# Retention matmuls in three rounded passes, a group norm split over three engines, and a merge projection that opens with a pair

## The chip, the cores and the metric

One core of a Trainium2 chip runs the whole layer. TensorE (PE) multiplies, VectorE (DVE) and ScalarE (ACT) do elementwise work, GpSimd (POOL) a little of it, and SyncE (SP) issues most of the DMAs. The metric is device time in microseconds (us) of one execution, lower is better. Three runs of the kernel before gave 1579.16, 1580.39 and 1580.98 us.

## The reference, cut to what matters

The layer works on 1024 positions of width 1024, in float32:

```python
h = rms_norm(x); proj = h @ w_in          # q, k, v, gates, two LRU branches, two merge gates
# branch A: retention, 4 heads, dk 128, dv 256; per chunk:
scores = (q_i @ k_i.T) * intra_decay
out    = scores @ v_i + (q_i * q_decay) @ state
state  = state * chunk_decay + (k_i * k_decay).T @ v_i
# per head: group norm over the 256 values of a position, times silu(gate), then @ w_ret_o
y = (o - mean(o)) * rsqrt(var(o) + GN_EPS)
# branch B: causal conv, RG-LRU (gates, scan), times gelu, then @ w_lru_o
mix = sigmoid(gA) * y_a + sigmoid(gB) * y_b
x = x + mix @ w_out                       # the merge projection
# gated MLP: h2 @ w_up (1024 x 6144), causal conv of width 3, gelu * val, @ w_down (3072 x 1024)
return rms_norm(x + ...)
```

The kernel handles two chunks of 64 positions as one block of 128, with a mask that holds the decays.

## The kernel before, in words

**Products.** The large products run with operands split by `split` (lines 465 to 471) into a rounded part and the rest, both of type float32r (written fp32r): ACT casts (L469), DVE subtracts (L470). A product of two split operands takes three passes, `PASSES = ((0, 0), (0, 1), (1, 0))`: high times high, high times low, low times high. A pass is one PE instruction, 128x512 in most places. On top of that the 2x2 blocks of a projection are multiplied by a Strassen-Winograd scheme: seven block products (`A11, S1, S2, A12, S3, A22, S4` against `B11, T1, T2, B21, T3, T4, B22`) instead of eight, at the price of sums of blocks on DVE. `mm_fast` does the seven (L718), `mm_by` does the plain eight (L680). A block product is 4 column groups of 3 passes, 12 instructions. A job with `mate` runs as a pair: each block of the right side is used by two jobs in turn.

**Stages.** First come the values of the retention heads (`values`, L1454), then the other input projections in the order of the string `SEQ`. The work on their results is written as generators (`back`, `builders`) that are advanced between block products: `rotary_head`, `retention_head` and `ret_out` for the heads, `lru_block` for branch B. Then follow the two output projections, the merge projection (`wjobs`, four jobs of 256 rows, `t` from 0 to 3), the up projection (`ups`) with its conv, and the down projection (`djobs`), whose last job ends in `final_half`.

**Retention.** Per head there are eight blocks. Each block makes three products in plain float32: scores transposed (L1233, 128x128), scores times values (L1239, 128x256) with the state's share added in the same bank (L1241), and, but for the last block, the state's update (L1250, 128x256). Between them DVE applies the mask (L1236) and the state's decay (L1254), ACT copies the result out (L1246). In the trace every float32 product stands as two PE instructions. After four blocks the group norm follows: DVE statistics (L1258, L1259), `rstd_of` (ACT square root L826, then a reciprocal and four small DVE operations with one Newton step), and one DVE operation per block that applies it (L1265).

**Merge projection.** Job `t=0` is plain (eight block products, by `mm_by` with the inner half as the outermost loop); the jobs 1 to 3 are fast. The right side is read in eight sets: the four blocks of `w_out` and the four sums, which an earlier stage left in DRAM as `tw_d`.

**Start and end.** The first eight columns of the parameters come by a DMA of POOL's queue (L1478), one tile of the input by ACT's queue, all else by SP's. Twelve matmuls on a zeroed tile `heat` run ahead (L1484). At the end the last quarter of the output is done in two halves of 256 columns by `final_half` (L1886 to L1906): a sum of squares (L1892), its addition (L1893), a multiplication by the norm's weights (L1894), then a power on POOL (L1897) and two scalings.

**What sets the order.** The program is built twice. The first build gives a list of instructions and their dependencies; the class `Plan` works out due times backward (`latest`), then picks instructions forward engine by engine (`forward`) with its own costs, and the second build is chained to that order. In `forward`, DVE and ACT may be left idle for an instruction that is soon ready (constants `NEAR`, `APART`).

Of the kernel before, what the change touches and what calls it, by code (L numbers as in the profile page):

```python
# [18 lines left out]
P = 128  # L19
# [180 lines left out]
class Plan:  # L200
# [8 lines left out]
    NEAR, APART = 500.0, 10000.0  # L209
# [97 lines left out]
    def forward(self, rank):  # L307
# [17 lines left out]
        while left:  # L325
# [100 lines left out]
def tile_trunk_layer(ctx, tc, x, xt, positions, params, consts, normf, w_in, w_v, w_ro, w_lo,  # L426
# [11 lines left out]
    sm = Units(pool, "sm", 4, [P, P], now)  # L438
# [386 lines left out]
    def rstd_of(dst, var, tmp):  # L825
        S.activation(tmp, var, AF.Sqrt)  # L826
        V.reciprocal(dst, tmp)
        V.tensor_mul(tmp, dst, dst)
        V.tensor_mul(tmp, tmp, var)
        V.tensor_scalar(tmp, tmp, -0.5, 1.5, ALU.mult, ALU.add)  # L830
        V.tensor_mul(dst, dst, tmp)

# [352 lines left out]
    def rotary_head(hd, qk):  # L1185
# [12 lines left out]
        for h in range(2):  # L1198
            ps = psa.get()
            for b in range(4):  # L1200
                bs = slice(128 * b, 128 * b + 128)
                PE.transpose(ps[:, bs], qk[1, h][:, bs], ident)
            t = get()
            for b in range(4):
                bs = slice(128 * b, 128 * b + 128)
                n = 4 * h + b
                S.activation(t[:, bs], ps[:, bs], AF.Copy, scale=kdr[:, hd, n:n + 1])
            psa.put(ps)
            kd[h] = t
            yield 0.5  # L1210
# [6 lines left out]
    def retention_head(hd, qk):  # L1217
        cur = 0
        tick = now[0]
        for g in range(2):  # L1220
            vt[0, g] = v_tile(hd, 0, g)
        yield from landed(tick)
        mask = cst[:, C_MASK + 128 * hd:C_MASK + 128 * hd + 128]
        for h in range(2):
            for b in range(4):
                if h == 0 and b % 2 == 0:
                    vt[1, b // 2] = v_tile(hd, 1, b // 2)
# [3 lines left out]
                v = vt[h, b // 2][:, 256 * (b % 2):256 * (b % 2) + 256]  # L1231
# [5 lines left out]
                psa.put(p1)  # L1237
                p2 = psa.get()
                PE.matmul(p2[:, 0:256], s, v, start=True, stop=first)  # L1239
                if not first:  # L1240
                    PE.matmul(p2[:, 0:256], qk[0, h][:, bs], rst[cur], start=False, stop=True)  # L1241
                sm.put(s)
# [168 lines left out]
    def values():  # L1411
# [74 lines left out]
        for j in (1, 2, 3):  # L1486
            wload("A11", j)
            xload("B11", j)
# [397 lines left out]
    def final_half(u, s):  # L1886
# [8 lines left out]
        if s.start == 0:  # L1895
            return
# [114 lines left out]
```

## Time and profile before

| | |
|---|---|
| runs | 1579.16, 1580.39, 1580.98 us (median 1580.39) |
| profiled execution | 1579.13 us, its span 1577.3 us |
| PE busy | 1566.6 us, 99% of the span, 7013 matmuls |
| DVE busy | 1373.0 us, 87% |
| ACT busy | 933.9 us, 59% |
| POOL busy | 52.6 us, 3% |
| granted clock of PE | 0.999 |

The profile is one execution. Its parts that are used below: the busy times by engine; groups of instructions by line and shape (count, busy time together, mean ns of one, and the idle time of the engine before them); the list of waits; the chain of work that ended last; the timeline; and busy times by stretch of the span. A matmul's shown duration is longer than its turn on PE, since matmuls overlap; its turn is read from the distance between starts, or from the busy time of a run of them.

### The profile page before, as it was taken

The numbers are of one execution on the slowest core, as the hardware profiler recorded it, in microseconds if no ns is written. First come the engines' busy times: TensorE is split into PE (matmuls) and PEld (weight loads), VectorE is DVE, ScalarE is ACT, GpSimd is POOL, SyncE is SP. The second block draws the span as 40 slices with busy tenths as digits, with TensorE's granted clock in tenths as the row PEclk, the third lists the DMA queues.
The fourth block names the chain that finished last, engine by engine and source line by source line (L and its number), as shares of the span: only waits on it lengthen the run. The fifth ranks groups of instructions, "written<-read, shape, count | busy, mean of one in ns | idle before, by whom it ended". The sixth has DMA issues, their size and how long they took to land.

```text
span 1577.3 us, 21478 instructions
## 1 busy us (share of the span) xinstructions
PE 1566.6 (99%) x7013; PEld 1294.2 (82%) x7013; DVE 1373.0 (87%) x2470; ACT 933.9 (59%) x1586; POOL 52.6 (3%) x74
## 2 busy tenths in 40 slices
PE   9999999999999999999999999999999999999998
PEld 7888888888888888888888888888888888888887
DVE  8999988898899888999997899777777778987885
ACT  7547964655567696955365764444444446563653
POOL 0001000000000000000000001000000000000000
PEclk9999999999999999999999999999999999999999
DMA  9344334444454245684996246444444456787752
GB/s 324 114 127 140 127 127 152 136 154 168 124 178 153 75 146 180 225 276 162 306 376 233 92 123 218 134 143 140 138 138 138 139 190 218 256 284 269 262 181 87
DMA packets 159328, 282.11 MB, mean 179 GB/s; under 512 B 17256, under 2 KB 29680, under 8 KB 159216
## 3 DMA queue, kind: packets, MB, share of 16 engines
q1 hardware_dynamic: 153664, 264.74, 51.1%
q0 software_dynamic: 4256, 13.64, 2.9%
q10 hardware_dynamic: 1296, 2.36, 0.4%
q8 instruction: 55, 0.90, 0.2%
q14 instruction: 57, 0.47, 0.1%
HBM read 195.73 MB, written 83.89 MB: 177 GB/s over the span
## 4 chain that ended last, share of the span: by engine, by line
PE 90%; DVE 4%; ACT 3%; DMA 1%; issue 1%; POOLq 0%; ACTq 0%; DVEq 0%; SPq 0%
PE g L718 78%; PE g L1454 5%; PE a L1130 2%; PE g L680 1%; DVE w L470 1%; PE a L1239 1%; PE a L1241 1%; PE a L1250 1%; PE a L1233 0%; PE a L1300 0%; DMA u<-td_d 0%; PE a L1720 0%; ACT u L469 0%; DMA u<-w_dn 0%; DMA w<-mix_d 0%
## 5 line engine op out<-in xcount | busy, mean ns | idle before, releaser
L718 PE MATMUL g<-u,w 128*128 128x512 f32 x5976 | 1390.1, 391 | 1.6 <-ACT u L767 1.5
L718 PEld LDWEIGHTS g<-u,w 128*128 128x128 f32 x5976 | 1115.2, 188 | 231.9 <-ACT u L767 3.5
L469 ACT CAST w<-w 128x512 fp32r<-128x512 f32 x516 | 316.6, 621 | 355.3 <-PE g L718 254.8
L470 DVE TENSOR_TENSOR w<-w,w 128x512 fp32r<-128x512 f32 x516 | 349.1, 682 | 63.3 <-ACT w L469 57.7
L747 DVE TENSOR_TENSOR u<-g,u 128x512 f32<-128x512 f32 x213 | 145.4, 684 | 52.9 <-PE g L718 43.7
L469 ACT CAST u<-u 128x512 fp32r<-128x512 f32 x233 | 138.4, 620 | 56.9 <-PE g L718 5.4
L767 ACT COPY u<-g 128x512 f32<-128x512 f32 x215 | 124.9, 582 | 61.6 <-PE g L718 59.4
L470 DVE TENSOR_TENSOR u<-u,u 128x512 fp32r<-128x512 f32 x233 | 152.8, 681 | 3.3 <-ACT u L469 2.8
L1769 DVE SCALAR_TENSOR_TENSOR u<-u,par,u 128x511 f32<-128x511 f32 x96 | 71.2, 743 | 2.9 <-ACT u L1766 2.6
L1454 PE MATMUL g<-w,u 128*128 128x512 f32 x264 | 61.9, 390 | 1.2 <-DVE u L1439 1.0
L1454 PEld LDWEIGHTS g<-w,u 128*128 128x128 f32 x264 | 49.3, 188 | 12.3 <-issue 1.5
L1774 POOL DMA_DIRECT2D ff_d<-u x48 | 36.1, 752 | 451.5 <-DVE u L1773 451.5
L1130 PE MATMUL a<-u,u 128*128 128x512 f32 x192 | 50.7, 393 | 0.3 <-ACT u L469 0.2
L555 DVE TENSOR_TENSOR w<-w,w 128x512 f32<-128x512 f32 x71 | 48.4, 682 | 1.4 <-DMA w<-w_lo 0.7
L558 DVE TENSOR_TENSOR w<-w,w 128x512 f32<-128x512 f32 x71 | 48.5, 684 | 0.9
L561 DVE TENSOR_TENSOR w<-w,w 128x512 f32<-128x512 f32 x71 | 48.4, 682 | 0.3
L564 DVE TENSOR_TENSOR w<-w,w 128x512 f32<-128x512 f32 x71 | 48.4, 682 | 0.3
L1766 ACT ACTIVATE u<-u,par 128x512 f32<-128x512 f32 x48 | 39.2, 816 | 16.0 <-DVE u L747 15.9
L741 DVE TENSOR_TENSOR u<-u,u 128x512 f32<-128x512 f32 x45 | 30.9, 686 | 16.9 <-ACT u L767 16.6
L1130 PEld LDWEIGHTS a<-u,u 128*128 128x128 f32 x192 | 35.5, 188 | 9.3 <-ACT u L469 1.3
L1773 DVE TENSOR_TENSOR u<-u,u 128x512 f32<-128x512 f32 x48 | 32.8, 686 | 6.1 <-ACT u L1772 6.1
L1112 DVE SCALAR_TENSOR_TENSOR u<-u,par,u 128x511 f32<-128x511 f32 (+2 forms) x48 | 35.7, 743 | 2.4 <-ACT u L1108 2.2
(211 smaller groups left out, 1130.4 us busy)
## 6 DMA issues: line engine op xcount, KB each, us to landing
w<-w_in SPq DMA_DIRECT2D x96, 256.0 KB, 2.7
w<-w_up SPq DMA_DIRECT2D x96, 256.0 KB, 2.7
u<-w_dn SPq DMA_DIRECT2D x84, 256.0 KB, 3.8
u<-x_d SPq DMA_DIRECT2D x60, 256.0 KB, 4.3
x_d<-u SPq DMA_DIRECT2D x48, 256.0 KB, 3.6
ff_d<-u POOLq DMA_DIRECT2D x48, 256.0 KB, 2.7
td_d<-u SPq DMA_DIRECT2D x48, 256.0 KB, 3.0
u<-td_d SPq DMA_DIRECT2D x48, 256.0 KB, 4.8
```

The costliest lines, as they stand in the source:

```text
L469: S.copy(hi, src)
L470: V.tensor_sub(lo, src, hi.bitcast(F32))
L555: V.tensor_add(s, r["A21"], r["A22"])
L558: V.tensor_sub(s, s, r["A11"])
L561: V.tensor_sub(s, r["A12"], s)
L564: V.tensor_sub(src, r["A21"], r["A11"])
L718: PE.matmul(bank[:, s], w[a][:, c], need(op, (SETS[nm], j))[b][:, s], start=first and n == 0, stop=n == 11, skip_group_check=True)
L747: V.tensor_add(u, bank, u)
L767: S.copy(u, bank)
L1130: PE.matmul(ps, wg[g][a][:, cs], xs[k][b], start=q == 0, stop=q == 5)
L1454: PE.matmul(bank, o[p][:, c], w[q], start=first and j == n == 0, stop=j == 3 and n == 2, skip_group_check=True)
L1769: V.scalar_tensor_tensor(c[:, s:], src[:, :TH - s], w, c[:, s:], ALU.mult, ALU.add)
```

## The change

1. In the retention, scores times values and the state's update take three rounded passes instead of one float32 product. For that the masked scores are split (128x128, per block), the values (four tiles per head) and the scaled keys (two tiles per head; the second half is made later, by the new `keys`). The scores themselves and the state's share stay in float32.
2. The group norm: `rstd_of` goes. POOL raises the variance to the power -0.5, DVE makes minus the mean times that, and ACT applies both as scale and bias.
3. The merge projection's first two jobs run as a fast pair in the order `FIRST`, and the right side is read in seven sets.
4. The first parameters and a second input tile go by ACT's queue; the zeroed tile is a unit of the common pool, given back after use.
5. In `final_half` the addition of the sum of squares is chained ahead of the multiplication by the weights.
6. The plan's rule for leaving DVE or ACT idle is another: an instruction is put off when a more urgent one gets ready before it would end.

```diff
@@ Plan.forward
-    NEAR, APART = 500.0, 10000.0
+    MARGIN, EXTRA = 600.0, 2000.0
             if e in ("DVE", "Activation"):
-                soon = min(((rank[n], at) for at, n in wait[e] if at < t + self.steps[item[1]].hold + self.NEAR),
-                           default=None)
-                if soon and soon[0] < min(t, item[0] - self.APART):
+                cost = self.steps[item[1]].hold
+                if e == "Activation" and switch(item[1]):
+                    cost += self.SWITCH
+                soon = min(((rank[n], at, self.steps[n].hold) for at, n in wait[e] if at < t + cost), default=None)
+                if soon and soon[0] < t + cost + self.MARGIN and item[0] > soon[1] + soon[2] + self.EXTRA:
                     free[e] = soon[1]
                     continue
@@ retention_head
+        def v_split(h, g):
+            t = raw.pop((h, g))
+            vt[h, g] = split(t)
+            put(t, late=SOONER)
...
+                s = s, *split(s, sm.get)
                 p2 = psa.get()
-                PE.matmul(p2[:, 0:256], s, v, start=True, stop=first)
+                for n, (i, j) in enumerate(PASSES):
+                    PE.matmul(p2[:, 0:256], s[1 + i], v[j][:, vs], start=n == 0, stop=first and n == 2)
...
-                    PE.matmul(p3[:, 0:256], kd[h][:, bs], v, start=True, stop=True)
+                    for n, (i, j) in enumerate(PASSES):
+                        PE.matmul(p3[:, 0:256], kd[h][i][:, bs], v[j][:, vs], start=n == 0, stop=n == 2)
...
-            rstd_of(rs[:, 1, :], rs[:, 0, :], rs[:, 2, :])
+            G.tensor_tensor(rs[:, 1, :], rs[:, 0, :], half[:, 0:4], ALU.pow)
+            V.scalar_tensor_tensor(rs[:, 2, :], mv[:, :, 0], -1.0, rs[:, 1, :], ALU.mult, ALU.mult)
             for b in range(4):
                 o = ob[h, b // 2][:, 256 * (b % 2):256 * (b % 2) + 256]
-                V.tensor_scalar(o, o, mv[:, b, 0:1], rs[:, 1, b:b + 1], ALU.subtract, ALU.mult)
+                S.activation(o, o, AF.Identity, bias=rs[:, 2, b:b + 1], scale=rs[:, 1, b:b + 1])
@@ keys (new; the loop over both halves stood in rotary_head)
+    def keys(hd, qk, h):
...
+        kd[h] = split(t)
+        put(t, late=SOONER)
@@ values
-        G.dma_start(par[:, 0:8], params[:, 0:8])
+        nc.scalar.dma_start(par[:, 0:8], params[:, 0:8])
         xload("B11", 0, nc.scalar)
+        xload("B11", 1, nc.scalar)
@@ merge projection
-        builders.append(operand(wop, w_out_set, False))
-        builders.append(kept_sums(wop, tw_d))
+        builders.append(operand(wop, kept_or(w_out_set, tw_d), False, ("B11", "T3", "B21", "T1", "T2", "T4", "B22")))
...
-                 emit_out(t, t > 0), out_post(t), fast=t > 0, last=t == 3, drop12=t == 0,
-                 pre=((0, 0), (0, 1), (1, 1)), fetch=from_x(t), by=None if t else "k",
-                 order=None if t else ("A11", "A21", "A12", "A22"),
+                 emit_out(t, True), out_post(t), fast=True, last=t == 3,
+                 pre=((0, 0), (0, 1), (1, 1)), fetch=from_x(t), mate=t == 0, prods=FIRST if t < 2 else PRODS,
@@ final_half
-        V.tensor_add(one, one, two)
-        V.tensor_mul(o[:, s], u[:, s], nf[1][:, s])
+        a = V.tensor_add(one, one, two)
+        b = V.tensor_mul(o[:, s], u[:, s], nf[1][:, s])
         if s.start == 0:
             return
+        tc.add_manual_dep(b.ins, a.ins.name, mybir.DependencyInfo(mybir.DependencyClass.NoSync,
+                          mybir.DependencyReason.DATA), reason="the sum first")
```

What the plan makes of it is shown at two places. PE in the first head, before: `a` are the two PSUM banks of the small products, `g` those of the projections, `sm` the masked scores.

```order
L1233 MATMUL a_89_2649<-u_417_2234,u_418_2271 128x128
L718 MATMUL g_79_2274<-u_268_860,w_427_2290 128x512
L718 MATMUL g_82_2337<-u_205_605,w_432_2310 128x512
L718 MATMUL g_82_2337<-u_206_606,w_432_2310 128x512
L718 MATMUL g_82_2337<-u_205_605,w_433_2311 128x512
L718 MATMUL g_82_2337<-u_209_614,w_432_2310 128x512
L1239 MATMUL a_91_2653<-u_437_2550,sm_15_2651 128x256
L1241 MATMUL a_91_2653<-state_87,u_417_2234 128x256
L1250 MATMUL a_93_2657<-u_437_2550,u_433_2498 128x256
```

The same block with the change (L1239 is now the scores, L1247 their product with the values, L1249 the state's share, L1259 the state's update, L720 the projections):

```order
L1239 MATMUL a_95_2749<-u_419_2234,u_420_2271 128x128
L720 MATMUL g_85_2441<-u_183_495,w_449_2375 128x512
L720 MATMUL g_85_2441<-u_182_494,w_450_2376 128x512
L720 MATMUL g_85_2441<-u_184_504,w_449_2375 128x512
L720 MATMUL g_85_2441<-u_185_505,w_449_2375 128x512
L720 MATMUL g_85_2441<-u_184_504,w_450_2376 128x512
L1259 MATMUL a_99_2764<-u_467_2705,u_461_2655 128x256
L1259 MATMUL a_99_2764<-u_468_2706,u_461_2655 128x256
L1259 MATMUL a_99_2764<-u_467_2705,u_462_2656 128x256
L1247 MATMUL a_97_2757<-u_467_2705,sm_44_2753 128x256
L1247 MATMUL a_97_2757<-u_468_2706,sm_44_2753 128x256
L720 MATMUL g_85_2441<-u_186_514,w_449_2375 128x512
```

The state's update moved ahead of the product that waits for the scores, and that product's third pass, which needs the low part of the scores (`sm_45`), stands one projection matmul later. ACT at the start of the program, before:

```order
L1430 DMA u_82_96<-xt 128x512
L1481 ACT_TABLE_LOAD
L1481 ACTIVATE st<-st 128x1
L469 CAST w_31_147<-w_23_98 128x512
L1512 ACTIVATE u_116_291<-u_82_96,par 128x512
```

And with the change:

```order
L1448 DMA u_83_96<-xt 128x512
L1496 DMA par<-params 128x8
L1448 DMA u_84_98<-xt 128x512
L1500 ACT_TABLE_LOAD
L1500 ACTIVATE st<-st 128x1
L471 CAST w_31_147<-w_23_100 128x512
L1533 ACTIVATE u_118_291<-u_83_96,par 128x512
```

The parameters' DMA stands behind the first input tile in ACT's queue, and a second input tile behind it. Over the whole program ACT's order holds 59 table loads where it held 72.

More of the change, by code (lines that the diff above doesn't have):

```diff
@@ L1197, in rotary_head @@
         yield from rest()
[L1198 to L1210, printed above, removed]
+        keys(hd, qk, 0)
+        yield 0.5
+    def keys(hd, qk, h):
+        ps = psa.get()
+        for b in range(4):
+            bs = slice(128 * b, 128 * b + 128)
+            PE.transpose(ps[:, bs], qk[1, h][:, bs], ident)
+        t = get()
+        for b in range(4):
+            bs = slice(128 * b, 128 * b + 128)
+            n = 4 * h + b
+            S.activation(t[:, bs], ps[:, bs], AF.Copy, scale=kdr[:, hd, n:n + 1])
+        kd[h] = split(t)
+        put(t, late=SOONER)
+        psa.put(ps)
     def v_tile(hd, h, g):
```

43 lines of the change are left out of this document (25 added, 18 removed).

## The prediction

> **What bounds the kernel now.** I read the page's busy times first, then PE's list of waits, then the busy times by stretch. The page:
>
> ```profile
> span 1577.3 us, 21478 instructions
> PE 1566.6 (99%) x7013; PEld 1294.2 (82%) x7013; DVE 1373.0 (87%) x2470; ACT 933.9 (59%) x1586; POOL 52.6 (3%) x74
> ```
>
> PE is busy for all but 10.7 us. A busy PE could still wait inside, so the list of PE's waits decides:
>
> ```profile
> PE g L718 <- ACT u L767: 1.5, 3, 0.8
> PE a L1484 <- DVE heat L1648: 1.3, 1, 1.3
> PE g L1454 <- DVE u L1439: 1.0, 1, 1.0
> PE a L1130 <- ACT u L469: 0.2, 1, 0.2
> ```
>
> These are total, times and longest: 4.0 us in all. The rest of the 10.7 is the start and the end. So the time is the number of PE's turns times the length of a turn. Work taken from DVE or ACT brings nothing by itself; work given to them costs only where they then come too late. How much room they have, by stretch (PE, PEld, DVE, ACT, POOL busy; the first four rows are the retention, the fifth the output projections, the last two the merge projection):
>
> ```profile
> 236.00:290.00 54.00, 54.00 (x261) 45.30 (x260) 46.62 (x108) 29.80 (x57) 0.00 (x0) 1.00 0.48 156
> 290.00:345.00 55.00, 55.00 (x264) 46.13 (x263) 49.82 (x113) 32.13 (x60) 0.00 (x0) 1.00 0.46 154
> 345.00:400.00 55.00, 55.00 (x264) 46.08 (x263) 48.95 (x111) 30.05 (x56) 0.00 (x0) 1.00 0.46 153
> 400.00:432.00 32.00, 32.00 (x155) 27.03 (x154) 25.91 (x70) 17.32 (x30) 0.00 (x0) 1.00 0.35 107
> 640.00:786.00 146.00, 146.00 (x646) 120.94 (x645) 144.67 (x240) 84.07 (x141) 0.00 (x0) 1.00 0.74 245
> 786.00:822.00 36.00, 34.70 (x152) 28.07 (x151) 31.17 (x52) 22.43 (x40) 0.00 (x0) 1.00 1.06 383
> 822.00:860.00 38.00, 38.00 (x171) 31.48 (x171) 31.16 (x57) 20.06 (x44) 1.80 (x2) 1.00 0.78 270
> ```
>
> In the retention DVE works 171.3 of 196 us and ACT 109.3. At 786 to 822 the DMA engines are full (share 1.06), and PE idles 1.3 us.
>
> **Retention products (gain).** The turn of a float32 product is read from the timeline of one block (start, duration):
>
> ```profile
> 241.14 0.59 PE L1239 MATMUL a<-u,sm 128*128 128x256 f32 x2
> 241.57 0.59 PE L1241 MATMUL a<-state,u 128*128 128x256 f32 x2
> 242.00 0.59 PE L1250 MATMUL a<-u,u 128*128 128x256 f32 x2
> ```
>
> Starts are 0.43 us apart, so one 128x256 product takes 0.43 us of PE. The trace has rounded passes of 256 columns too, in the last down projection:
>
> ```profile
> L718 PE MATMUL g<-u,w 128*128 128x256 f32 x24 | 3.0, 283 | 0.0
> L718 PEld LDWEIGHTS g<-u,w 128*128 128x128 f32 x5976 | 1115.2, 188 | 231.9 <-ACT u L767 3.5
> ```
>
> 24 of them end to end: (3.0 - 0.283)/23 = 0.118 us a turn, weights changing as they will in the retention. Three take 0.355, so each product saves 0.075. It is done for 32 products of scores and 28 updates (the trace's 64 of L1239 and 56 of L1250 are two instructions each): 60 x 0.075 = 4.5 us. The ends: rounding of the 3.0 gives 0.116 to 0.120, so 4.2 to 4.9. A change of dtype between neighbours costs something too, but scores and the state's share stay float32, so there are as many changes as before; I take nothing.
>
> The Trainium skill, "TensorE: Matmul & The Clock Gate", section "Back-to-back issue gap", gives N/2.4 + 2.5 ns: 109 ns for 256 columns, by which this term would be 6.2 us. The measured rows of this kernel are longer, so the trace decides.
>
> **Retention's operands (on DVE and ACT, hidden).** Rows for the prices:
>
> ```profile
> L470 DVE TENSOR_TENSOR u<-u,u 128x512 fp32r<-128x512 f32 x233 | 152.8, 681 | 3.3 <-ACT u L469 2.8
> L469 ACT CAST u<-u 128x512 fp32r<-128x512 f32 x233 | 138.4, 620 | 56.9 <-PE g L718 5.4
> L1236 DVE SCALAR_TENSOR_TENSOR sm<-a,rcol,cst 128x128 f32<-128x128 f32 x32 | 11.0, 345 | 2.0 <-PE a L1233 1.6
> L1207 ACT ACTIVATE u<-a,kdr 128x128 f32<-128x128 f32 x32 | 10.5, 370 | 1.6 <-DVE u L1285 0.8 <-PE a L1202 0.6
> L1265 DVE TENSOR_SCALAR u<-u,mv,rs 128x256 f32<-128x256 f32 x32 | 11.2, 406 | 0.0
> L827 DVE RECIPROCAL rs<-rs 128x4 f32<-128x4 f32 x8 | 1.4, 172 | 1.1 <-ACT rs L826 1.0
> L1766 ACT ACTIVATE u<-u,par 128x512 f32<-128x512 f32 x48 | 39.2, 816 | 16.0 <-DVE u L747 15.9
> L826 ACT ACT_TABLE_LOAD x8 | 10.3, 1283 | 0.1
> ```
>
> Splits of keys and values are 6 a head, 24: DVE 24 x 152.8/233 = 15.7 us, ACT 24 x 138.4/233 = 14.3. Splits of the scores, 32 of 128x128: at most the rows of that size, 0.34 on DVE and 0.33 on ACT, 11 and 10.5 us. The norm takes L1265's 11.2 us from DVE and five small operations each half head (40 x about 0.17 = 6.8), and gives back 8 small ones (1.4). Net at most 15.7 + 11.0 - 11.2 - 6.8 + 1.4 = 10 us on DVE, of 24.7 idle. ACT gets 32 scalings of 256 columns, each between 0.37 and 0.82, I take 0.55, 18 us; it loses 13 table loads of 1.283, 16.7 us. Net about 26 of 87 idle. Both fit, so PE pays nothing on the sum; without that cover the 10 us of DVE would be PE's.
>
> What is queued behind: the scaling on ACT waits for POOL's power, and casts and evacuations behind it wait along. POOL's rows of this operation:
>
> ```profile
> L1692 POOL TENSOR_TENSOR nst<-nst,half 128x2 f32<-128x2 f32 x4 | 3.6, 904 | 748.9 <-DVE nst L1691 748.9
> L958 POOL TENSOR_TENSOR rcol<-nst,half 128x8 f32<-128x8 f32 x1 | 2.6, 2646 | 65.9 <-DVE nst L957 65.9
> ```
>
> Four columns lie between, about 1.5 us, eight times. No projection matmul waits for the norm; its reader is `ret_out`'s transposes (L1300), in banks of their own.
>
> **Merge projection (gain).** Eight block products become seven in job 0: 12 instructions of 128x512. Their turn, from the chain (start, length, count):
>
> ```profile
> 643.70 142.71 PE g L718 x630
> ```
>
> 142.71/630 = 0.2265, so 2.7 us. The pair needs two sets of left blocks early: four `mix_d` tiles, four of `w_out` and four of `tw_d` ahead of its first 48 matmuls, where two and eight did. Over the stage SP's queue reads four tiles fewer. DVE gets three splits and four sums more for job 0's blocks (4.7 us) and four operand splits fewer (2.6), of 11.7 idle in the two last stretches. With the DMA full there, the unknown is how PE's 1.3 us of idling changes: gone at best, doubled at worst. I take no change.
>
> **Start (gain).**
>
> ```profile
> 1.27 4.42 DMA par<-params
> 0.74 0.41 ACTq L1430 DMA_DIRECT2D u<-xt  x1
> u<-xt ACTq DMA_DIRECT2D x1, 256.0 KB, 3.7
> 4.23 0.62 ACT L469 CAST w<-w 128x512 fp32r<-128x512 f32 x1 [1.55 <-DMA w<-w_v]
> 1.25 4.06 PE L1484 MATMUL a<-heat 128*128 128x512 bf16 x12 [1.25 <-DVE heat L1648]
> 6.35 9.98 PE L1454 MATMUL g<-w,u 128*128 128x512 f32 x41 [1.03 <-DVE u L1439]
> ```
>
> POOL's DMA of the parameters lands at 5.69; the input tile by ACT's queue lands at 0.74 + 3.7 = 4.4, the weights at 4.2. The parameters now go out right behind that tile, so I put them at 4.5 to 4.9. PE's warm-up ends at 5.31 and cannot be passed by more than DVE's first 0.6 us allows: PE starts at about 5.4 instead of 6.35. I take 0.9 us; the ends are 0.3 (parameters late by 0.6) and 1.1.
>
> **End (gain).**
>
> ```profile
> 1571.91 0.34 DVE u L1894
> 1572.25 0.08 DVE nst L1893
> ```
>
> The last chain has L1894 ahead of the addition that POOL waits for. Turned round, it loses 0.34; the multiplication then lies beside the power. I take 0.3.
>
> **The plan's rule (no price).** Where the second half of the program is concerned (up and down projections), order of PE, DVE and ACT is nearly the old one. Elsewhere it decides only how PE's 4 us of waits change. I take nothing; the ends are 2 us less and 5 more.
>
> **Sum.** 4.5 + 2.7 + 0.9 + 0.3 = 8.4 us. The profiled execution took 1579.13, so it would take 1570.7. The median of the runs is 1580.39, 1.26 above that execution; the forecast for the median is 1572.0 us. About 0.2%, 3.2 us, is what a measurement here can tell from no change.
>
> **Rivals.**
>
> 1. *The retention's chain gets too long.* Before, scores to product is one DVE operation under five projection matmuls (5 x 0.2265 = 1.13 us). Now it is L1236, a cast on ACT (0.33) and a subtraction on DVE (0.34), under those five and three update passes (1.13 + 0.355 = 1.49). The cover grows by 0.36 for the product's first two passes, which need the cast alone; the third has 0.6 to 0.7 more with one matmul more (0.23). Against it: no wait is listed today in the retention. For it: both queues are in order, and a 0.68 us operation ahead of either half breaks the cover. At 0.15 us in each of 32 blocks it costs 4.8: 1576.8.
> 2. *The plan lets DVE stand idle where it is full* (slower). At 640 to 786 DVE is busy 144.67 of 146 us. If in that stretch every tenth of its 240 operations is held for 0.6 us, near the length of one, DVE loses 14 us that it hasn't got, and PE waits for split blocks: 1572.0 + 14 = 1586. It decides from 11.6 us on, where the gain is eaten and 3.2 more. Against it: the order there is close to the old one.
> 3. *DVE is locked while POOL raises to the power.* If a DVE operation with two inputs blocks for the 1.5 us, eight powers cost up to 12 us of DVE, at worst all on the chain of rival 1: 1584. But beside the long power of before DVE's operations keep their length:
>
> ```profile
> 67.86 2.65 POOL L958 TENSOR_TENSOR rcol<-nst,half 128x8 f32<-128x8 f32 x1 [65.89 <-DVE nst L957]
> 68.29 0.68 DVE L470 TENSOR_TENSOR u<-u,u 128x512 fp32r<-128x512 f32 x1
> 69.55 0.68 DVE L470 TENSOR_TENSOR w<-w,w 128x512 fp32r<-128x512 f32 x1
> ```
>
>    The Trainium skill, "SBUF — State Buffer", section "Who interferes with whom", states such a lock: with two inputs in SBUF a DVE operation and a GpSimd one that reads SBUF exclude each other, and the later one fully blocks. By that rule DVE should have stood still during those 2.65 us; the trace does not show it.
> 4. *The passes don't pay.* A weight load shows 188 ns, more than a 256-column pass. If every pass took that, three would take 0.564 against 0.43, and 60 of them cost 8 us: 1580.4 - 3.9 + 8.0 = 1584.5. The row of 24 passes at 0.118, each with its own load, speaks against it.
>
> **How the numbers follow.** Forecast 0.74 (1568.5 to 1575.5), rival 1 0.12 (1575.5 to 1579), rival 2 0.07, rival 3 0.04, rival 4 0.03. The low end is all waits of before that can go gone (2 more, with 1.3 of the merge stage): 1568.5. The high end takes in rival 1: 1578.5. What is left out is rivals 2 to 4 and the tails, under 0.2. Faster by over 0.2% (below 1577.2): 0.74 and most of rival 1, 0.84. Within 0.2%: 0.07. Slower: 0.09.
>
> **What would show it.** Right: the products at L1247 and L1259 with starts 0.12 apart; PE's first L1472 near 5.4 us; no L680; the list of PE's waits still a few us. Wrong: waits of PE for DVE or ACT in the retention (rival 1), PE waiting at 640 to 786 with DVE idle (rival 2), DVE operations of 1.5 us and more beside POOL's powers (rival 3), starts of passes 0.19 apart (rival 4).

## The result and the profile after

| | before | after |
|---|---|---|
| runs, median (lowest to highest) | 1580.18 us (1578.81 to 1582.20) | 1576.99 us (1576.29 to 1579.56) |
| ratio of after to before | | 0.9981, 95% interval 0.9975 to 0.9987 |
| profiled execution, its span | 1579.13, 1577.3 us | 1576.54, 1574.8 us |
| PE busy | 1566.6 us | 1561.6 us |
| DVE, ACT, POOL busy | 1373.0, 933.9, 52.6 us | 1382.9, 954.1, 63.3 us |

The change is faster by 3.2 us, where 8.4 were forecast; the time lies in the stated range, well above its middle. Two executions measured with the experiments below ran at a granted clock of 0.77 and 0.71 and took 1916 and 2088 us; no figure here uses them. The page of the kernel after, its span and busy times:

```profile
span 1574.8 us, 21660 instructions
PE 1561.6 (99%) x7061; PEld 1289.4 (82%) x7061; DVE 1382.9 (88%) x2472; ACT 954.1 (61%) x1655; POOL 63.3 (4%) x81
```

PE's list of waits after (total, times, longest):

```profile
PE g L720 <- ACT u L769: 2.5, 4, 1.3
PE a L1503 <- DVE st L1671: 1.5, 1, 1.5
PE g L720 <- ACT w L471: 1.3, 1, 1.3
PE a L1742 <- ACT a L1701: 0.5, 1, 0.5
PE a L1259 <- DVE u L472: 0.3, 1, 0.3
PE g L720 <- ACT u L471: 0.3, 1, 0.3
```

6.4 us where 4.0 were. The wait on the warm-up's zeroes (L1503) went from 1.3 to 1.5; the rest of the increase is waits for ACT. The same stretches as before (PE, PEld, DVE, ACT, POOL busy; clock, DMA share, GB/s):

```profile
345.00:400.00 55.00, 54.69 (x282) 46.04 (x281) 49.97 (x108) 32.50 (x68) 3.78 (x2) 1.00 0.42 133
...
640.00:786.00 146.00, 145.28 (x641) 119.99 (x640) 143.73 (x238) 83.27 (x139) 0.00 (x0) 1.00 0.75 246
786.00:822.00 36.00, 33.39 (x145) 26.70 (x144) 34.19 (x57) 23.48 (x43) 0.00 (x0) 1.00 0.97 338
822.00:860.00 38.00, 37.52 (x168) 30.81 (x167) 33.67 (x62) 20.45 (x44) 2.16 (x2) 1.00 0.80 262
```

The last three rows are the output and merge projections: PE idles 0.72, 2.61 and 0.48 us, 3.81 together, where it idled 1.30 in one of them. The increase of 2.5 us lies at the end of the output projections and in the merge projection.

**Where the time went.** The trace lets the same piece of work be found in both kernels: the k-th projection matmul, that is, the k-th PE instruction into a bank `g`. I compare the starts of four of them and split each difference in two: turns (how many instructions of each kind lie between, at 0.2267 us for a pass of 512 columns, 0.1195 for a rounded one of 256, 0.4304 and 0.2166 for a float32 product of 256 and 128 columns, each kind's median distance between starts) and loss (the rest, that is, time in which PE stood still or ran slower).

| stretch | after minus before | of it turns | of it loss | forecast |
|---|---|---|---|---|
| start to the 500th projection matmul | +0.72 | 0 | +0.72 | -0.9 |
| 500th to 2900th: last input projections, retention, output projections | -3.63 | -4.31 | +0.68 | -4.5 |
| 2900th from the front to 2900th from the end: merge projection | +0.74 | -2.72 | +3.46 | -2.7 |
| from there to the last: up and down projections | -0.49 | 0 | -0.49 | 0 |
| last projection matmul to the end of the span | +0.10 | | | -0.3 |
| sum | -2.56 | | | -8.4 |

(The third row compares 608 projection matmuls before with 596 after. From here on it is called the merge stage; it begins at 764 us, in the last output job.) The turns went as forecast, 7.0 us of 7.2. What failed is what was to come from waits: 4.4 us came back as loss, most of it in the merge projection, and the start and the end gave nothing.

**The retention.** One block after, from the timeline:

```profile
244.21 0.52 PE L1259 MATMUL a<-u,u 128*128 128x256 f32 x3
244.30 0.28 DVE L472 TENSOR_TENSOR sm<-sm,sm 128x128 fp32r<-128x128 f32 x1
...
244.56 0.40 PE L1247 MATMUL a<-u,sm 128*128 128x256 f32 x2
244.80 0.63 PE L720 MATMUL g<-u,w 128*128 128x512 f32 x2
```

Three passes take 244.56 - 244.21 = 0.35 us, two 0.24: about 0.12 each (the medians over all are 0.118 at L1259 and 0.119 at L1247). DVE's split of the scores ends at 244.58, beside them. No wait stands here. Over the four heads no product at L1247 waits for a split; updates at L1259 do, for 0.3 us in PE's list above.

**The merge projection.** ACT and PE at the first stall after:

```profile
783.59 0.62 ACT L471 CAST u<-u 128x512 fp32r<-128x512 f32 x1 [1.55 <-DMA u<-w_out]
...
784.29 0.62 ACT L471 CAST w<-w 128x512 fp32r<-128x512 f32 x1
...
784.81 0.58 ACT L769 COPY u<-g 128x512 f32<-128x512 f32 x1
...
785.45 4.62 PE L720 MATMUL g<-u,w 128*128 128x512 f32 x19 [0.72 <-ACT u L769]
```

The copy L769 frees the bank that PE needs. It stands in ACT's queue behind a cast that waited 1.55 us for a tile of `w_out` on its way, and one more. The chain of work that ended last shows how far this reaches, after:

```profile
785.61 3.72 DMA u<-w_out
789.33 0.68 DVE u L1418
...
796.06 0.70 DVE u L1419
796.78 4.80 DMA mix_d<-u
802.49 5.21 DMA w<-mix_d
807.72 0.63 ACT w L471
```

Before, it ran through PE alone to 786.4 and through one transfer and ACT to 793.8:

```profile
786.41 5.49 DMA w<-mix_d
...
791.97 0.61 ACT w L469
...
793.14 0.59 ACT u L767
```

After, the last mixing on DVE (L1418, L1419), the store of `mix_d` and its reading back follow each other until 808, where PE waits 1.3 us for the cast. Releasers are inferred in this view: the step from the `w_out` tile to L1418 is not a dependency of the kernel, and DVE was busy ahead of it.

**The start and the end.** Start, after:

```profile
5.98 0.72 ACT L1533 ACTIVATE u<-u,par 128x512 f32<-128x512 f32 x1 [0.81 <-DMA par<-params]
6.00 0.49 DVE L1457 TENSOR_SCALAR u<-u,par 128x512 fp32r<-128x512 f32 x1 [4.55 <-DMA par<-params]
```

The first operations on the parameters start at 5.98 us, 0.27 later than in the profiled execution before (5.71). At the end the addition of the sum of squares now stands first, and POOL's power starts 1.23 us after DVE takes up the last bank (1568.36 to 1569.59), where it took 1.44 (1571.02 to 1572.46):

```profile
1568.36 0.42 DVE L737 TENSOR_TENSOR u<-g,u 128x256 f32<-128x256 f32 x1
...
1569.29 0.16 DVE L1913 TENSOR_TENSOR nst<-nst 128x1 f32<-128x1 f32 x1
1569.37 0.42 DVE L1914 TENSOR_TENSOR u<-u,u 128x256 f32<-128x256 f32 x1
1569.59 0.59 POOL L1919 TENSOR_TENSOR nst<-nst,half 128x1 f32<-128x1 f32 x1 [1.71 <-DVE nst L1913]
```

### The profile page after: what moved, and what is told of

It is laid out like the page before. It is cut to its first block, busy times and chain, and to the rows that moved or that the text cites. A ratio compares the mean times of both kernels' runs of the same rounds, so it can differ in the third digit from the quotient of the medians.

```text
span 1574.8 us, 21660 instructions
## 1 busy us (share of the span) xinstructions
PE 1561.6 (99%) x7061; PEld 1289.4 (82%) x7061; DVE 1382.9 (88%) x2472; ACT 954.1 (61%) x1655; POOL 63.3 (4%) x81
## 4 chain that ended last, share of the span: by engine, by line
PE 45%; DVE 4%; DMA 2%; issue 1%; ACT 1%; SPq 0%; POOLq 0%; DVEq 0%; ACTq 0%
PE g L720 44%; DVE w L472 1%; DVE u L472 1%; DMA mix_d<-u 1%; DVE u L1419 0%; PE a L1742 0%; DMA u<-sg_d 0%; DMA w<-mix_d 0%; DMA x_d<-u 0%; DVE u L749 0%; DVE u L1418 0%; DMA u<-x 0%; DMA u<-w_out 0%; DVE w L560 0%; DVE w L563 0%
## 5 line engine op out<-in xcount | busy, mean ns | idle before, releaser
L720 PE MATMUL g<-u,w 128*128 128x512 f32 x6060 | 1414.7, 391 | 4.1 <-ACT u L769 2.5
L720 PEld LDWEIGHTS g<-u,w 128*128 128x128 f32 x6060 | 1129.2, 188 | 236.0 <-ACT u L769 4.5
L471 ACT CAST u<-u 128x512 fp32r<-128x512 f32 x253 | 150.3, 620 | 55.2 <-PE g L720 5.3
L769 ACT COPY u<-g 128x512 f32<-128x512 f32 x218 | 126.8, 582 | 79.8 <-PE g L720 72.9
L472 DVE TENSOR_TENSOR u<-u,u 128x512 fp32r<-128x512 f32 x253 | 166.4, 682 | 1.4 <-ACT u L471 1.2
L1789 DVE SCALAR_TENSOR_TENSOR u<-u,par,u 128x511 f32<-128x511 f32 (+1 forms) x96 | 71.3, 745 | 2.9 <-ACT u L1786 2.6
```

The costliest lines, as they stand in the source:

```text
L471: S.copy(hi, src)
L472: V.tensor_sub(lo, src, hi.bitcast(F32))
L720: PE.matmul(bank[:, s], w[a][:, c], need(op, (SETS[nm], j))[b][:, s], start=first and n == 0, stop=n == 11, skip_group_check=True)
L769: S.copy(u, bank)
L1789: V.scalar_tensor_tensor(c[:, s:], src[:, :TH - s], w, c[:, s:], ALU.mult, ALU.add)
```

## The experiments

The first question was which part brings what. The loss in the merge stage is worked out as in the table above, from each kernel's profiled execution. That is one execution: for the retention alone it was the quickest of eleven (1577.70 us), for the pair alone the slowest (1581.23). It shows where the time goes; what a kernel is worth is read from the medians.

**The retention alone.**

```diff
 (kernel before, and of the change only)
+ three passes for scores times values and the state's update, splits, norm on POOL and ACT
```

> The kernel before with the retention's and the norm's part alone (rounded passes, splits, new keys, power on POOL, scaling on ACT; the zeroed tile a unit of the pool, of which 256 columns are set). Plan rule, start, merge projection and end as before. Theory A (the turns saved are as forecast, part is given back as waits around the retention): 4.5 us saved, 0.5 to 1 given back, 1576.5 us. Theory B (the plan's new rule for idling makes the waits): the old rule gives nothing back, 1575.7 us or less. If the norm on POOL and ACT itself disturbs, 1578 or more.

Measured: 1579.40 us, ratio to before 1.0002 [0.9993, 1.0010]: no gain. The turns are gained as in the whole change, but from the 1300th to the 1700th projection matmul, the end of the retention, 4.5 us are lost, where before lost 1.3 and after 2.4. Two places make 2.4 of the 4.5, 1.55 and 0.84 (by starts). This execution is 1.7 us under the median, and where the others lose that is not shown. ACT and PE at the larger place in this kernel:

```profile
453.03 0.82 ACT L1108 ACTIVATE u<-u,par 128x512 f32<-128x512 f32 x1 [3.23 <-DVE u L1072]
453.86 1.28 ACT L1341 ACT_TABLE_LOAD   x1
...
455.16 0.72 ACT L1341 ACTIVATE u<-u,par 128x512 f32<-128x512 f32 x1
455.79 0.56 ACT L767 COPY u<-g 128x512 f32<-128x512 f32 x1
...
456.40 0.98 PE L718 MATMUL g<-u,w 128*128 128x512 f32 x3 [1.39 <-ACT u L767]
```

A table load and a sigmoid stand ahead of the copy that frees PE's bank. In the kernel after the copy stands ahead of the table load. PE loses nothing at the same matmul (the 1680th), and 0.2 us twelve matmuls later by its list of waits:

```profile
451.30 0.82 ACT L1102 ACTIVATE u<-u,par 128x512 f32<-128x512 f32 x1 [4.25 <-DVE u L1066]
452.02 0.57 ACT L769 COPY u<-g 128x512 f32<-128x512 f32 x1
452.60 1.28 ACT L1335 ACT_TABLE_LOAD   x1
```

**The pair alone.**

```diff
 (kernel before)
-        builders.append(operand(wop, w_out_set, False))
-        builders.append(kept_sums(wop, tw_d))
+        builders.append(operand(wop, kept_or(w_out_set, tw_d), False, ("B11", "T3", "B21", "T1", "T2", "T4", "B22")))
...
+                 ... fast=True, mate=t == 0, prods=FIRST if t < 2 else PRODS,
```

> The kernel before with the merge projection's part alone (first two jobs as a fast pair, seven sets). Theory A (the pair saves 2.7 us of turns and waits take it all back, because evacuations on ACT stand behind casts that wait for DMAs in a stage with full DMA): 0 to 1 us slower than before, 1580.2 to 1581.2. Theory B (the waits come of the plan's new rule): 2.7 us faster, 1577.5.

Measured: 1579.35 us, ratio 0.9998 [0.9989, 1.0007]. The loss in the merge stage is 6.3 us where before had 3.3: the pair gives back its 2.7 us of turns without any help from the other parts. (This execution loses 1.3 us more in the up and down projections too, at 1348 us for the most part, which is no part of the merge stage.)

**The change with the merge projection of before.** The reverse of the diff above, in the kernel after.

> The changed kernel with the merge projection of before (first job plain, eight sets). Theory A: 0.7 us faster than the changed kernel, 1576.3, with PE's waits between 780 and 910 us back at about 2.5 us. Theory B, and the forecast on record: 2.7 us of turns lost, 1579.7.

Measured: 1576.72 us, ratio 0.9981 [0.9972, 0.9990], the same as after. Loss in the merge stage 2.95 us. With this and the one before, the pair is worth nothing that can be measured in either surroundings.

**The change with the plan's rule of before.**

```diff
-    MARGIN, EXTRA = 600.0, 2000.0
+    NEAR, APART = 500.0, 10000.0
...
-                if soon and soon[0] < t + cost + self.MARGIN and item[0] > soon[1] + soon[2] + self.EXTRA:
+                if soon and soon[0] < min(t, item[0] - self.APART):
```

> The changed kernel with the plan's rule of before. Theory A: the waits at the merge projection and in the retention stay, within 1 us of the changed kernel, 1576 to 1578. Theory B: the waits go, 1572 to 1573.

Measured: 1578.82 us, ratio 0.9993 [0.9984, 1.0002], against 0.9981 [0.9975, 0.9987] with the new rule; the intervals overlap at their ends. The end of the retention loses 5.3 us, and the same two places cost 1.55 and 0.84 again. So the rule that I gave no price is worth about 1.8 us here, and the trace puts it at the new retention: ACT's table load is put off when the copy is soon ready. The rule alone in the kernel before was not run, so what it would do for the old retention is not shown.

The second question was the start and the merge stage's loss.

**The start of before.**

```diff
-        nc.scalar.dma_start(par[:, 0:8], params[:, 0:8])
+        G.dma_start(par[:, 0:8], params[:, 0:8])
...
-        xload("B11", 1, nc.scalar)
...
-    V.memset(warmth, 0.0)
+    V.memset(warmth[:, 0:TH // 2], 0.0)
```

> The changed kernel with the start of before: the parameters by POOL's queue, one input tile by ACT's queue, and a zeroing of 256 columns instead of 512 ahead of the warm-up. Theory 'the start lost time' (the parameters queue behind an input tile of 256 KB in ACT's queue and land at 5.98 instead of 5.69; the zeroing is 0.2 us longer): the first projection matmul goes from 6.63 back to 6.35 us, the 0.27 us stall behind it goes, time 0.4 to 0.7 us less than the changed kernel's. Rival 'the parameters don't set the start' (the wait is for the operations on DVE and ACT behind them): the first projection matmul stays at 6.6, time the same within 0.2 us.

Measured: 1577.08 us, ratio 0.9984 [0.9975, 0.9993], no other than after. The first projection matmul starts at 6.63 us as in after: the rival's case. The start scatters from one execution to the next: with the parameters on POOL's queue the first projection matmul started at 6.35 (before), 6.41 (the pair alone), 6.63 and 6.72 (the retention alone); with them behind an input tile on ACT's queue at 6.63 (after) and 6.56 to 6.93 in the other kernels. The first operations on the parameters began at 5.71, 5.78, 6.00 and 6.08 by POOL's queue, so 5.98 is no later than these. The new start is some 0.2 us later by the means, with ranges that overlap, and not 0.9 earlier.

**The parameters first.**

```diff
         nc.scalar.dma_start(par[:, 0:8], params[:, 0:8])
-        xload("B11", 0, nc.scalar)
+        xload("B11", 0)
         xload("B11", 1, nc.scalar)
...
-    V.memset(warmth, 0.0)
+    V.memset(warmth[:, 0:TH // 2], 0.0)
```

> The changed kernel with the parameters first in ACT's queue, one input tile behind them, the other input tile by SP's queue, and a zeroing of 256 columns. Theory 'the start lost time since the parameters are behind an input tile': they land by 4 us, the first projection matmul starts between 5.4 and 5.9 us instead of 6.63, time 0.7 to 1.2 us less. Rival 'the input tiles set the start as well': the tiles land later than before, the first projection matmul starts at 6.3 or later, time less by 0.3 us at most.

Measured: 1573.66 us (1573.08 to 1574.68), ratio 0.9960 [0.9947, 0.9972]: 3.3 us under after (0.9981, the intervals apart), the quickest kernel of all, and for another reason than I expected. Its start:

```profile
5.95 0.49 DVE L1457 TENSOR_SCALAR u<-u,par 128x512 fp32r<-128x512 f32 x1 [1.22 <-DMA u<-xt]
...
6.58 2.08 PE L1472 MATMUL g<-w,u 128*128 128x512 f32 x8 [1.21 <-DVE u L1457]
```

Now the input tile lands last, and PE starts at 6.58: the input tiles set the start as well. But the plan answers the moved transfers with another order on PE, DVE, ACT and SP, down to the merge projection. By the starts of the same matmuls this kernel is 0.65 us ahead of after at the 500th projection matmul, 0.41 at the 2900th, and 3.65 behind the merge projection, where it loses 3.5 us instead of 6.7. The kernel with the start of before is the control: its order is that of after on all these engines from 12 us on, and its merge stage loses 6.5. So the 3 us go with the new order and not with the start itself. In the merge stage ACT's order differs. After, and then with the parameters first, the same copy (at 790.76 us after, at 788.09 here) and what stands ahead of it:

```
L769 COPY u_1513_8128<-g_223_8000 128x512
L471 CAST w_1366_8145<-w_1365_8143 128x512
L471 CAST u_1563_8211<-u_1500_8100 128x512
L471 CAST u_1585_8245<-u_1529_8159 128x512
L471 CAST u_1593_8257<-u_1537_8171 128x512
L471 CAST u_1607_8294<-u_1554_8197 128x512
L471 CAST u_1555_8199<-u_1498_8096 128x512
L471 CAST u_1581_8239<-u_1525_8153 128x512
L769 COPY u_1567_8217<-g_223_8000 128x512
```

```
L769 COPY u_1513_8128<-g_223_8000 128x512
L471 CAST w_1355_8082<-w_1335_8001 128x512
L471 CAST u_1593_8257<-u_1537_8171 128x512
L471 CAST w_1366_8145<-w_1365_8143 128x512
L471 CAST u_1585_8245<-u_1529_8159 128x512
L471 CAST u_1563_8211<-u_1500_8100 128x512
L471 CAST u_1607_8294<-u_1554_8197 128x512
L769 COPY u_1567_8217<-g_223_8000 128x512
L471 CAST u_1555_8199<-u_1498_8096 128x512
L471 CAST u_1581_8239<-u_1525_8153 128x512
```

Two casts that stood ahead of the copy now stand behind it; the first of them had waited 0.63 us for a tile of `tw_d` on its way. Another cast has come in ahead, so that the copy stands behind six instead of seven. DVE's and SP's order differ too, so this one row is not shown to be the cause.

**The right side read earlier.**

```diff
-    ojobs[-2].post = out_start
+    ojobs[-3].post = out_start
```

> The changed kernel, with the reads and splits of the merge projection's right side released one output job earlier. Theory 'head of line' (evacuation copies of the last output job stand in ACT's queue behind casts that wait for a block of w_out or a sum still on its way): the blocks come earlier, PE's stalls at 784 and 790 us (2.4 us together) fall under 1 us, the stall at 806 (a mix_d tile on its way) stays near 1.4; time 1 to 2 us less. Rival 'the DMA engines are full whatever the order': the reads push others back, the stalls move but their sum stays within 0.7 us of the changed kernel's, time the same.

Measured: 1577.33 us, ratio 0.9983 [0.9975, 0.9992]. The stalls at 784 and 790 are gone, and one of 4.0 us stands at 803, where PE waits for a cast of a `mix_d` tile; three stalls of 3.8 us together have become one. The rival holds: the stalls move, and their sum stays. The loss is 7.4 us for one more reason, which shows in the clock (the column before the DMA share):

```profile
805.00:825.00 20.00, 17.52 (x71) 14.37 (x72) 18.35 (x31) 9.82 (x19) 0.00 (x0) 0.91 0.87 286
```

From 807.16 to 810.57 us the trace grants PE half its clock, and passes start 0.427 us apart. That costs another 1.6 us. After the shorter stalls of the kernel after the same stretch has a clock of 1.00. One long stall thus cost more here than three short ones of the same sum.

**The evacuation on DVE.**

```diff
-                    S.copy(u, bank)
+                    (V.tensor_copy if jb in ojobs[-2:] + wjobs[:2] else S.copy)(u, bank)
```

> The changed kernel with the evacuation copies of the last two output jobs and of the merge pair on DVE instead of ACT. Theory 'head of line': the copies no longer stand behind casts that wait for a transfer, so PE's stalls at 784 and 790 us (2.4 us together) fall under 1 us; the one at 806 stays; time 1 to 2 us less, if DVE, with about 10 us of idle time left in these stretches, can take 16 or more copies. Rival 'DVE is full there': the sums and subtractions come later, the stalls move to 'PE waits for DVE' and the time is the same or up to 3 us more.

Measured: 1577.74 us, ratio 0.9985 [0.9976, 0.9994]. The stalls at 784 and 790 fall from 2.4 to 1.3 us, others of 1.3 and 0.4 appear at 803 and 801; the loss is 7.1 us. Taking the copies out from behind the casts moved PE's waits and did not shorten the loss.

**A quarter of the bytes.**

```diff
+            G.memset(t[:, 128:TH], 0.0)
-            SY.dma_start(t, src[int(n[1]) - 1, j])
+            SY.dma_start(t[:, 0:128], src[int(n[1]) - 1, j][:, 0:128])
 (and the same for w_out)
```

> The changed kernel with the 28 tiles of the merge projection's right side read from DRAM only in their first 128 of 512 columns; POOL zeroes the rest, so a quarter of the bytes of w_out and of its sums is read and the values are left out, while every matmul, cast, subtraction and copy stays. Theory 'transfers arrive late': what PE waits for in the merge stage is in the end a tile on its way, and ACT's order only decides which one; with 5.5 MB less to move the time over the nominal turns in this stage falls from 6.7 us to 3 or less, and the time to 3 us or more under the changed kernel's. Rival 'ACT's and DVE's order': the same casts and copies stand in nearly the same order and cost the same, so it stays at 5.5 to 7 us and the time within 1 us of the changed kernel's.

Measured: 1628.37 us, ratio 1.0305 [1.0291, 1.0320]. This run decides nothing: the zeroing put POOL's queue into the path. The group of its memsets (idle time before them last) and the busiest stretch of the stall:

```profile
L1377 POOL MEMSET u<- 128x384 f32 x16 | 6.1, 418 | 35.0 <-DVE u L472 23.6 <-DMA u<-w_out 6.1 <-PE g L720 3.9
```

```profile
805.00:825.00 20.00, 12.09 (x39) 9.03 (x40) 12.67 (x20) 9.93 (x18) 4.02 (x11) 0.76 0.20 69
```

POOL waits in order for a tile to come free before each memset, the reads wait for POOL, and PE stands still with the DMA engines at 0.20. The granted clock is 0.76 in that stretch, so a part of the loss is half clock.

**More bytes.** The test from the other side.

```diff
 (and the new DRAM tile `two_d`)
+            if ch % 2 == 0:
+                G.dma_start(*(d[2 * h:2 * h + 2, :, ch // 4, :, ch % 4, :].rearrange("t m p c -> p (t m) c")
+                              for d in (two_d, mix_d)))
```

> The changed kernel with eight more transfers ahead of and in the merge projection: every second tile of mix_d, once stored, is copied by POOL's queue to another place in DRAM, 256 KB each, and nothing reads or waits for the copies; the order on PE, ACT and DVE stays all but the same. Theory 'transfers arrive late' (the DMA engines are full at 765 to 805 us and the blocks that the casts wait for come later when more is in flight): 2.1 MB more at 350 to 390 GB/s is 5 to 6 us of the engines' time, and PE's stalls in the merge stage grow by 3 to 6 us. Rival 'the order on ACT and DVE alone decides': the stalls keep their lengths, time the same within 0.7 us.

Measured: 1578.98 us, ratio 0.9993 [0.9984, 1.0002], 2.0 us over after. PE's list of waits leads with

```profile
PE g L721 <- ACT w L472: 3.2, 1, 3.2
PE g L721 <- ACT u L770: 2.1, 4, 0.9
```

The first is the wait at 806 us for a `mix_d` tile, 1.3 us in after; the loss is 8.5 us, 1.8 more. PE's order is the same but for three places behind 857 us, and nothing waits for the copies. DVE's and SP's orders differ at some thirty and some two dozen places between 770 and 855 us, ACT's at eleven, and the intervals of the two ratios overlap at their ends. So more traffic went with more loss, as the theory says, but this run does not part the traffic from the order. The increase is below the 3 to 6 us expected; the DMA share at 805 to 825 was 0.88 in after and is 0.97 here, so there was room for a part of the added transfers.

**The quickest kernel with the merge projection of before.** The reverse of the pair's diff, in the kernel with the parameters first.

> The kernel with the parameters first (1573.7 us, the quickest so far) with the merge projection of before. Theory 'the pair is worth its 2.7 us of turns once its waits are no longer than those of before': with the parameters first the merge stage ran 3.5 us over its turns with the pair; without it the 12 matmuls come back and the waits stay near 3, so time 1.5 to 3 us more, 1575.2 to 1576.7. Rival 'the pair is worth nothing in any order': the time is the same within 0.7 us.

Measured: 1574.88 us (1573.52 to 1578.48), ratio 0.9966 [0.9952, 0.9980] against 0.9960 [0.9947, 0.9972] with the pair. The pair looks worth 1.2 us here, less than its turns, and the intervals don't tell it from nothing. The profiled execution was the longest of its five (1578.48, where the others took 1573.52 to 1575.22), and shows a long wait:

```profile
787.95 0.62 ACT L471 CAST w<-w 128x512 fp32r<-128x512 f32 x1 [0.31 <-DMA w<-mix_d]
...
789.96 0.62 ACT L471 CAST u<-u 128x512 fp32r<-128x512 f32 x1 [1.38 <-DMA u<-w_out]
791.43 0.62 ACT L471 CAST u<-u 128x512 fp32r<-128x512 f32 x1 [0.86 <-DMA u<-w_out]
791.96 0.58 ACT L769 COPY u<-g 128x512 f32<-128x512 f32 x1
...
792.59 0.73 PE L720 MATMUL g<-u,w 128*128 128x512 f32 x2 [3.87 <-ACT u L769]
```

Three casts ahead of the copy wait for their tiles in turn, and PE waits 3.87 us for a copy of 0.58. Here too half the clock follows, from 793.95 to 797.37 us (0.66 in the mean of 793 to 798), and costs another 1.6. The two together make 5.5 of the 6.5 us that this execution loses in the merge stage. The quicker executions left no trace, so that they lack this wait is likely, not shown.

**One number of the rule.**

```diff
-    MARGIN, EXTRA = 600.0, 2000.0
+    MARGIN, EXTRA = 300.0, 2000.0
```

> The changed kernel with one number of the plan's rule halved (MARGIN 300 for 600), which moves rows on every engine and no work. Theory 'the order's details decide the merge stage': its time over the nominal turns comes out other than the changed kernel's 6.7 us by more than 1 us, either way, and the run's time moves by 1 to 3 us. Rival 'the transfers decide whatever the order': 6 to 7.5 us again, time the same within 0.7 us.

Measured: 1576.13 us (1574.77 to 1577.31), ratio 0.9977 [0.9968, 0.9986], which lies within noise of the 0.9981 of after. In the profiled execution the merge stage loses 4.5 us instead of 6.7, the stretch from the 500th to the 2900th matmul 2.3 us more than in after. So the time tells the theory from the rival no better than its noise; the stage itself moved by 2.2 us, which speaks for the order.

Taken together, the loss of the merge stage with the pair was 6.3 to 7.4 us in six kernels, 4.5 and 3.5 in two with another order, and 8.5 with more traffic; with the old merge projection 3.0 to 3.3 in three, and 6.5 in the execution with the long wait. That the pair costs waits is shown by the pair alone and by its removal; how much it costs hangs on the order of the other engines' work.

## Why the prediction was right or wrong, step by step

- **Retention products: right.** Forecast -4.5; the turns changed by -4.3, since a pass takes 0.118 to 0.120 us, the upper end of what the 24 passes of before gave. That nothing was taken for changes of type holds within what the loss shows.
- **Retention's operands, hidden: right in sum, not in order.** DVE rose from 171.3 to 176.7 us in the four stretches (10 at most expected), ACT from 109.3 to 123.0 (26 expected). But "both fit, so PE pays nothing on the sum" overlooks that a sum cannot show one copy behind a table load: with the old rule that cost PE 2.4 us at two places (1.55 and 0.84 in the trace of the retention alone), and with the new one the whole stretch from the 500th to the 2900th matmul loses 0.7 more than before.
- **Merge projection: wrong, the largest step.** The turns are the 2.72 us of the forecast. "Gone at best, doubled at worst. I take no change" was the failing step: PE's idling in the three last stretches nearly tripled (1.30 to 3.81), and by starts the loss rose by 3.46, so that the term came out at +0.74 instead of -2.7. The pair alone and the change without it say the same by the medians: worth nothing. I had a likely cause in hand, twelve tiles ahead of the first 48 matmuls where ten did with the DMA share at 1.06, and priced it at zero because the traffic in sum fell. The traces show PE waiting for copies and casts that stand behind tiles on their way, in the end for the `mix_d` tile stored last. That the two more tiles make these waits is not shown: no run changed their number alone, and other orders of the same work lost 3.5 and 4.5 us.
- **Start: wrong.** "I put them at 4.5 to 4.9" was read from a queue that holds one tile; the work on them began at 5.98, where it began at 5.71 before and at 6.00 with the start of before put back. Even with the parameters first, an input tile landed at 5.95 and PE started at 6.58. The low end of the term, a gain of 0.3, did not hold either: it came out at a loss of 0.28 in the two profiled executions. A further 0.4 us is lost near 32 us; it is not there with the old rule.
- **End: not seen in the time.** POOL's power starts 0.21 us earlier after DVE takes up the last bank, against the 0.3 taken, but the span from the last matmul on is 0.1 us longer: the output's last transfers took 3.8 us from the issue instead of 3.5. This span scatters from 6.62 to 6.90 us in the three kernels with the old end and from 6.29 to 6.74 in the eleven with the new one, so a gain of 0.2 would not stand out.
- **The plan's rule: wrong at zero.** It is worth about 1.8 us. The end "2 us less" of its range was where it came out; the place is not the waits of before but the ones that the change itself would have made.
- **Rival 1, the retention's chain:** not where it was put. No block waits for the split scores. The loss in that stage is 0.7 us, against its 4.8. The measured time lies in this rival's band (1575.5 to 1579), but by another path.
- **Rival 2, DVE idle at 640 to 786:** DVE was busy 143.73 us against 144.67, PE lost 0.72 there. The rule shortens the time.
- **Rival 3, DVE locked beside POOL's powers: not seen.** At the longest power:

```profile
363.34 2.49 POOL L1277 TENSOR_TENSOR rs<-rs,half 128x4 f32<-128x4 f32 x1 [36.83 <-DVE rs L1276]
```

```profile
363.68 0.69 DVE L566 TENSOR_TENSOR w<-w,w 128x512 f32<-128x512 f32 x1
364.28 0.69 DVE L472 TENSOR_TENSOR w<-w,w 128x512 fp32r<-128x512 f32 x1
```

  DVE's operations with two inputs keep their 0.69 us while the power runs; the power is the one that varies, 1.01 to 2.49 us over the eight. The lock that the Trainium skill, "SBUF — State Buffer", section "Who interferes with whom", describes is not shown by these runs. Whether POOL waits for DVE instead they do not show either.
- **Rival 4, passes at the weight load's length:** starts 0.12 apart, so no.

What stays open: which single difference in order makes the merge stage lose 3.5 us rather than 6.7 with the parameters first. Moving the copies or the reads alone did not do it, and the lower traffic could not be tried without a new wait. Open is also what the new rule is worth without the new retention.

## What to carry to other kernels

A gain in turns on a full engine is not yet a gain in time. The merge projection, with the DMA engines at a share of 1.06, gave 2.7 us of turns back as waits; the retention kept most of its 4.3 us, but only with the rule that kept a table load from standing ahead of a copy. Where a change needs more tiles landed before its first instructions, ask by when each must have landed, and not only how many bytes the stage moves; the first stalls here were waits for such tiles. Before the order of an engine's queue is given a price of zero, look for short operations that free another engine's buffer and ask what long or waiting operation can come to stand ahead of them: a copy of 0.58 us behind three casts cost 3.87. And count one long stall higher than several short ones: after the two of about 4 us half the clock cost 1.6 us more.

## What the runs showed of the hardware

- A 4 KB transfer issued at 1.18 us behind a 256 KB tile on ACT's queue was in use at 5.98, after 4.8 us; by POOL's queue it was in use 4.4 and 4.7 us after its issue (1.27 to 5.71 before, 1.27 to 6.00 with the start of before put back). Whatever was moved among the first transfers, the first work on the last one needed began at 5.71 to 6.00 us in the four starts looked at.
- A rounded pass of 256 columns takes 0.118 to 0.120 us, a little more than half of the 0.2267 of 512 columns.
- A power of four columns on POOL took 1.01 to 2.49 us over eight times, with one shape.
- One order of instructions ran from 1573.52 to 1578.48 us in five executions of the same kernel; the profile of the longest shows a single wait of 3.87 us for tiles on their way.
- After PE's waits of 3.87 us in two kernels (the right side read earlier, and the quickest kernel with the merge projection of before) the trace grants half the clock for 3.41 us, with passes of 512 columns 0.427 us apart instead of 0.227. After the wait of 3.2 us in the kernel with more bytes, and the one of 1.33 in after, the clock stays at 1.00.
